# Attention scores of 64-feature heads: three half-height matmuls replaced by two full-height ones

## The chip, the cores and the metric

The kernel runs on one core of a Trainium2 chip. The metric is device time in microseconds (us) for one execution. The engines are named as in the profile: PE is TensorE (its weight loads are listed as PEld), DVE is VectorE, ACT is ScalarE, POOL is GpSimd, and SP is SyncE, whose queue issues the DMAs. All five run side by side, each works through its own instruction list strictly in the order written at build time, and semaphores make one wait for another.

## The reference, cut to what matters

Two blocks follow each other on 256 tokens of width 1024. The first block has two layers. Each layer projects the tokens (and 256 context tokens) with `w_in` and computes three kinds of attention, A, B and C. A has 32 features per head; B and C have 64, and they are what the change touches:

```
qb = axial_rope(rms_norm(qb.reshape(b, s, B_HEADS, HEAD_DIM), gqa_q_norm[l]), row, col)
kb = axial_rope(rms_norm(kb.reshape(b, s, B_KV_HEADS, HEAD_DIM), gqa_k_norm[l]), row, col)
yb = map_query_blocks(lambda q_blk: gqa_attend(q_blk, kb_all, vb_all), qb) * jax.nn.silu(gb)
qn = rms_norm(qn.reshape(b, s, C_HEADS, HEAD_DIM), nat_q_norm[l])
kn = rms_norm(kn.reshape(b, s, C_HEADS, HEAD_DIM), nat_k_norm[l])
yn = neighbourhood_attend(qn, kn, vn.reshape(b, s, C_HEADS, HEAD_DIM), kn_c, vn_c, nat_rpb[l], rows)
```

In layer 0 the context tokens attend too (to the context keys alone); in layer 1 they give only keys and values. B has six query heads on two key heads, C has six heads with a bias table `nat_rpb`. The second block (a gated MLP and a dilated attention) isn't touched.

## The kernel before

**Tiling.** Tokens come in four blocks of 128: blocks 0 and 1 are the tokens x, blocks 2 and 3 the context c. The columns of `w_in` are cut into seven slabs of 512 per layer: slabs 0 and 1 hold two A heads each, slabs 2 and 3 three B heads with their one key head, slabs 4 to 6 two C heads each. For each slab the code projects the blocks (`project`, which calls `mm3`) and then attends (`attend`), one block after the other. In layer 0 the loads and matmuls of `ada`, which make modulation vectors from `w_ada`, are spread between the slabs.

**Precision.** A 32-bit operand is held as a high part (rounded to the matmul's format) and a low part, the rest. A product takes three matmuls: high by high, low by high, high by low. `mm3` (L193 to L195) does so for the projections, at full height, that is with 128 rows of contraction. `scores` (L331) does so for one or two heads at a time, on the 64 rows where a head's features lie; two heads of a pair lie on rows 0 to 63 and 64 to 127 of the same tile.

**A projection's way to the scores.** `project` copies the matmul's result to `pj` (L472), makes the normalization factor on POOL (L202, L204), splits the values (`split_v`, L298 to L302), scales (L496), applies gains or the rotary tables (`times_tab`, L430 and L437, then L507), and has the result in `fin`. For B a POOL copy (L511) sets the key head a second time beside itself. Then two transposes (L517; three for a full B block) put features on rows, ACT casts the high parts out of PSUM (L522) and DVE subtracts to get the low parts (L523). A B slab's third query head has a tile of its own, `qx`, with one buffer, whose tag `aux` the C slabs' bias `rpb` shares.

**Softmax.** Two PSUM banks (`sc`) hold scores. DVE takes the maximum (L566; for C L560 and L561, which adds the bias), ACT exponentiates (L313) and rounds (L318), DVE makes the low part (L319), a DMA transposes the result (L321, tile `pt`), and PE multiplies with the values (L339 to L341).

**What sets the order.** In the first block a scheduler decides at build time in which order each engine gets its instructions; `urgent(40)` on `scores` raises their priority. The order is fixed when the kernel runs. Tiles with the same tag share their buffers, so a tile waits until the last use of the one whose buffer it takes.

**Tables.** The cosine and sine tables are loaded once, ahead of layer 0 (L673), and POOL multiplies them with the gains at the start of each layer (L705). `gates_of` loads the residual gate for a layer's output projection into a buffer of its own (`rowb`).

## Time and profile before

| | |
|---|---|
| time, median of 3 runs | 1182.47 us (1181.87 to 1186.19) |
| the profiled execution | 1193.97 us, of which 1192.3 us are its span |
| mean granted TensorE clock in it | 0.954 of full speed |
| PE busy | 1113.6 us (93%), 6600 matmuls |
| DVE, ACT, POOL busy | 837.6 us (70%), 610.5 us (51%), 465.8 us (39%) |
| the chain that ended last | 79% PE, 10% DMA, 5% DVE |
| score matmuls (L331) on that chain | 7% |

A busy time counts overlapping instructions of one engine once. A PE matmul's duration in the trace includes its latency, so how fast matmuls follow each other is read from their starts, not from their durations. The first block takes the span up to about 680 us; B and C slabs lie in about 178 to 400 us (layer 0) and 534 to 650 us (layer 1).

### The profile page before, as it was taken

How to read it: one execution, taken by the hardware profiler on the slowest of the kernel's cores; microseconds unless marked ns; L12 is line 12 of the kernel's file. 1: busy time of each engine (PE TensorE's matmuls, PEld its weight loads, DVE VectorE, ACT ScalarE, POOL GpSimd, SP SyncE). 2: the span in 40 equal slices, each digit the busy share in tenths (PEclk: the TensorE clock that was granted, in tenths of full speed). 3: DMA queues.
4: the chain of work that ended last, by engine and by line, in shares of the span. 5: the costliest groups of instructions: out<-in, count | busy, mean ns of one | idle time of the engine just before them, and what ended most of it. 6: DMA issues, size and time to landing. Idle time of an engine off the chain costs nothing.

```text
span 1192.3 us, 19339 instructions
## 1 busy us (share of the span) xinstructions
PE 1113.6 (93%) x6600; PEld 851.7 (71%) x6600; DVE 837.6 (70%) x1833; ACT 610.5 (51%) x1364; POOL 465.8 (39%) x698
## 2 busy tenths in 40 slices
PE   5988999898999989999997899999999999999996
PEld 1656657465676777777775688888778888888885
DVE  4467777775476677768876559765568888888783
ACT  2445564554364555566654354554446545555551
POOL 3476655341451039354361301000255555555520
PEclk9989989996999999789999899999989999999998
DMA  9355665878495535666766475555457666876652
GB/s 354 140 146 105 162 146 107 221 141 221 134 235 138 147 128 159 125 106 140 171 161 149 158 245 183 191 170 183 137 179 196 173 178 185 192 173 184 170 144 63
DMA packets 193971, 197.88 MB, mean 166 GB/s; under 512 B 150448, under 2 KB 154576, under 8 KB 193616
## 3 DMA queue, kind: packets, MB, share of 16 engines
q1 hardware_dynamic: 193872, 196.65, 62.0%
q8 instruction: 52, 0.85, 0.3%
q14 instruction: 47, 0.39, 0.1%
HBM read 158.84 MB, written 2.11 MB: 135 GB/s over the span
## 4 chain that ended last, share of the span: by engine, by line
PE 79%; DMA 10%; DVE 5%; issue 2%; ACT 2%; POOL 1%; SPq 0%; DVEq 0%; POOLq 0%; ACTq 0%
PE pj L193 17%; PE pj L194 17%; PE pj L195 16%; PE sc L331 7%; DMA pt<-pp 5%; PE ops L194 3%; PE ops L193 3%; PE ops L195 3%; PE po_bank L339 3%; DMA raw<-in_w_ada 2%; PE po_bank L341 2%; PE adaps L391 2%; DVE wlo L177 1%; PE po_bank L340 1%; PE tp L517 1%
## 5 line engine op out<-in xcount | busy, mean ns | idle before, releaser
L193 PE MATMUL pj<-whi,hxh 128*128 128x512 f32 (+1 forms) x800 | 317.3, 397 | 5.2 <-ACT hxh L271 4.3
L194 PE MATMUL pj<-whi,hxl 128*128 128x512 f32 (+1 forms) x800 | 309.6, 387 | 1.1 <-DVE hxl L255 0.7
L195 PE MATMUL pj<-wlo,hxh 128*128 128x512 f32 (+1 forms) x800 | 307.5, 384 | 0.0
L172 ACT CAST whi<-raw 128x1024 fp32r<-128x1024 f32 x224 | 235.0, 1052 | 139.8 <-DMA raw<-in_b_w_qk 32.5
L175 POOL TENSOR_TENSOR wlo<-raw,whi 128x512 fp32r<-128x512 f32 x130 | 181.6, 1418 | 149.6 <-ACT whi L172 146.5
L177 DVE TENSOR_TENSOR wlo<-raw,whi 128x1024 fp32r<-128x1024 f32 x159 | 202.2, 1275 | 53.5 <-ACT whi L172 52.1
L193 PEld LDWEIGHTS pj<-whi,hxh 128*128 128x128 f32 x800 | 154.3, 193 | 38.4 <-ACT hxh L271 5.0
L194 PEld LDWEIGHTS pj<-whi,hxl 128*128 128x128 f32 x800 | 154.3, 193 | 32.5 <-issue 2.6
L195 PEld LDWEIGHTS pj<-wlo,hxh 128*128 128x128 f32 x800 | 153.4, 192 | 30.3 <-issue 1.1
L313 ACT ACTIVATE pe<-sc,nm 128x512 f32<-128x512 f32 (+2 forms) x184 | 105.3, 576 | 106.9 <-DVE nm L566 51.9
L319 DVE SCALAR_TENSOR_TENSOR pp<-pe,pp 128x512 f16<-128x512 f32 (+3 forms) x152 | 114.8, 760 | 43.4 <-ACT pp L318 42.8
L331 PE MATMUL sc<-qk 64*128 64x256 f32 (+4 forms) x612 | 107.8, 355 | 4.6 <-ACT qk L522 1.9
L318 ACT ACTIVATE pp<-pe 128x512 f16<-128x512 f32 (+3 forms) x152 | 88.6, 590 | 43.2 <-DMA pt<-pp 42.4
L204 POOL TENSOR_TENSOR rs<-ms,mhalf 128x1 f32<-128x1 f32 (+3 forms) x98 | 92.4, 944 | 4.2
L331 PEld LDWEIGHTS sc<-qk 64*128 64x128 f32 (+1 forms) x612 | 64.3, 191 | 39.1 <-issue 13.9
L339 PEld LDWEIGHTS <-pt 128*128 128x128 f16 x544 | 54.0, 99 | 47.0 <-issue 23.2
L193 PE MATMUL pj<-whi,hch 128*128 128x512 f32 (+2 forms) x224 | 81.9, 367 | 0.5 <-ACT whi L172 0.5
L194 PE MATMUL pj<-whi,hcl 128*128 128x512 f32 (+2 forms) x224 | 81.6, 365 | 0.4 <-DVE hcl L255 0.4
L195 PE MATMUL pj<-wlo,hch 128*128 128x512 f32 (+2 forms) x224 | 80.2, 363 | 0.0
L339 PE MATMUL po_bank<-vt,pt 128*128 128x128 bf16 x400 | 67.5, 228 | 13.4 <-DMA pt<-pp 10.4
L341 PE MATMUL po_bank<-vt,pt 128*128 128x128 bf16 x400 | 66.9, 226 | 0.0
L566 DVE TENSOR_REDUCE nm<-sc 128x1 f32<-128x512 f32 (+1 forms) x96 | 54.1, 573 | 18.1 <-PE sc L331 17.6
(192 smaller groups left out, 1963.5 us busy)
## 6 DMA issues: line engine op xcount, KB each, us to landing
raw<-in_b_w_qk SPq DMA_DIRECT2D x64, 512.0 KB, 4.3
raw<-in_w_in SPq DMA_DIRECT2D x56, 512.0 KB, 4.6
raw<-in_w_ada SPq DMA_DIRECT2D x48, 512.0 KB, 4.9
raw<-in_a_w_in SPq DMA_DIRECT2D x48, 512.0 KB, 4.7
raw<-in_w_out SPq DMA_DIRECT2D x16, 512.0 KB, 4.4
raw<-in_a_w_out SPq DMA_DIRECT2D x16, 512.0 KB, 4.6
raw<-in_b_w_vz SPq DMA_DIRECT2D x16, 512.0 KB, 4.1
raw<-in_b_w_out SPq DMA_DIRECT2D x8, 512.0 KB, 3.9
```

The lines of the kernel that those rows point to most:

```text
L172: nc.scalar.copy(hi, raw)
L175: nc.gpsimd.tensor_tensor(lo[:, j], raw[:, j], hi[:, j].bitcast(F32), ALU.subtract)
L177: nc.vector.tensor_tensor(lo, raw, hi.bitcast(F32), ALU.subtract)
L193: nc.tensor.matmul(ps, h, whi[:, c0:c1], start=st, stop=False)
L194: nc.tensor.matmul(ps, l, whi[:, c0:c1], start=False, stop=False)
L195: nc.tensor.matmul(ps, h, wlo[:, c0:c1], start=False, stop=en)
L204: nc.gpsimd.tensor_tensor(rs[:, :n], ms[:, :n], mhalf[:, :n], ALU.pow)
L313: nc.scalar.activation(pe[:, c : c + w], ps, AF.Exp, bias=nm, scale=sign, accum_out=zz)
L319: nc.vector.scalar_tensor_tensor(pp[:, 1, :], pe, PSCALE, pp[:, 0, :], ALU.mult, ALU.subtract)
L331: nc.tensor.matmul(o, q[i == 2], k[i == 1], start=(i == 0), stop=(i == 2))
L339: nc.tensor.matmul(ps, pt[:, 0, i, :], v[:, 0:128], start=(i == 0), stop=False)
L341: nc.tensor.matmul(ps, pt[:, 1, i, :], v[:, 0:128], start=False, stop=(i == n - 1))
```

## The change

**Scores.** For B and C, `project` doubles each head's 64 features side by side before the transposes: ACT copies `fin` into the 512 columns of `pj`, each head twice (L531 of the new file). A transpose of 128 columns then gives one head on rows 0 to 63 and the same head on rows 64 to 127. There is one transpose per head (L533): four for a full block, one or two for a block that gives keys alone. ACT casts all of it out of PSUM (L534). For a key head DVE subtracts on all 128 rows (L535), so that the low part, tile `kl`, stands on both halves too. For a query head DVE subtracts on rows 64 to 127 alone (L538), so that the high part stands above the low part. `scores2` (L336 and L337) then multiplies this query tile by the keys' high parts and by their low parts, two matmuls of 128 rows, where there were three of 64. The fourth product, low by low, comes in with them. A keeps its form.

**Memory.** `qx` and the POOL copy L511 are gone; `kl` is new, with two buffers. To make room the rotary products work in place in `fin`, the cosine and sine tables are loaded in each layer into a shared `s512` buffer (L720), and the gate of `gates_of` shares the tag `aux` with the bias `rpb`.

In the built program the counts are: 216 score matmuls of 64 rows become 144 of 128 rows (of 512 columns 144 become 96, of 256 columns 72 become 48); 110 transposes become 164; ACT has 40 doubling copies more (30 of them 128x512), and 30 casts of 128x512 in place of ones of 128x256 and 128x128; DVE's subtractions there go from 68 to 86; POOL loses 16 copies; SP has four table loads in each layer in place of four in all.

```
-                qk = [wk.tile([P, 4, 2, P], F32R, tag="qk" + t, bufs=2, name="qk") for t in "hl"]
+                qk = wk.tile([P, 4, 4, P], F32R, tag="qk", bufs=2, name="qk")
                 qx = None
-                if kd == "B":
-                    qx2 = wk.tile([P, 2, 4, P], F32R, tag="aux", bufs=1, name="qx")
-                    qx = [qx2[:, i] for i in range(2)]
+                if kd == "A":
...
+                else:
+                    qx = wk.tile([P, 4, 1 if kd == "B" else 2, P], F32R, tag="kl", bufs=2, name="kl")
...
-                if kd == "B":
-                    nc.gpsimd.tensor_copy(fin[:, 256:320], fin[:, 192:256])
-                wins = (0, 192, 128) if kd == "B" else (0, 128)
...
+                nq = qw // 64
+                i0 = 0 if full else nq
+                two = pj.rearrange("p (h t d) -> p h t d", h=4, t=2)[:, i0:4]
+                heads = fin[:, 64 * i0 : 256].rearrange("p (h d) -> p h d", d=64)
+                nc.scalar.copy(two, heads.unsqueeze(2).to_broadcast([P, 4 - i0, 2, 64]))
+                for i in range(i0, 4):
+                    nc.tensor.transpose(tp[:, i, :], pj[:, i * P : (i + 1) * P], ident)
+                nc.scalar.copy(qk[:, blk, i0:4, :], tp[:, i0:4, :])
+                nc.vector.tensor_tensor(qx[:, blk], tp[:, nq:4, :], qk[:, blk, nq:4, :].bitcast(F32), ALU.subtract)
+                if full:
+                    ql = qk[64:128, blk, 0:nq, :]
+                    nc.vector.tensor_tensor(ql, tp[64:128, 0:nq, :], ql.bitcast(F32), ALU.subtract)
...
+    @urgent(40)
+    def scores2(o, q, kh, kl):
+
+        nc.tensor.matmul(o, q, kh, start=True, stop=False)
+        nc.tensor.matmul(o, q, kl, start=False, stop=True)
...
+                        if kd != "A":
+                            q = qk[:, blk, r0, :]
+                            scores2(
+                                sc_[:, :nk], q, qk[:, kb0:4, (192 if kd == "B" else 128) // 64 + vh, :], qx[:, kb0:4, vh, :]
+                            )
+                            continue
...
-                    scr.tile([P, D], F32, tag="rowb", bufs=1, name="gtb"), gd[l][i].rearrange("k p -> (k p)")
+                    wk.tile([P, D], F32, tag="aux", bufs=1, name="gtb"), gd[l][i].rearrange("k p -> (k p)")
...
-            for nm, w in (("cosA", 32), ("sinA", 32), ("cosB", 64), ("sinB", 64)):
-                t = tb_.tile([P, 2, w], F32, name=nm)
-                nc.sync.dma_start(t, a[nm])
-                consts[nm] = t
...
+                tabs, consts = {}, {}
+                cs4 = s512("cs").rearrange("p (t a d) -> p t a d", t=4, a=2)
+                for i, (nm, w) in enumerate((("cosA", 32), ("sinA", 32), ("cosB", 64), ("sinB", 64))):
+                    consts[nm] = cs4[:, i, :, :w]
+                    nc.sync.dma_start(consts[nm], a[nm])
```

**PE, layer 1, the heads of the second B slab's block 1.** Before, one of the pair's heads stands alone between projection matmuls (`pj<-`):

```order
L193 MATMUL pj<-whi,hxh 128x512
L194 MATMUL pj<-whi,hxl 128x512
L195 MATMUL pj<-wlo,hxh 128x512
L331 MATMUL sc<-qk 128x512 x3
L193 MATMUL pj<-whi,hxh 128x512
```

After, the pair's second head and the slab's third head at the same place:

```order
L336 MATMUL sc<-qk 128x512
L337 MATMUL sc<-kl,qk 128x512
L336 MATMUL sc<-qk 128x512
L337 MATMUL sc<-kl,qk 128x512
L193 MATMUL pj<-whi,hxh 128x512
```

Three matmuls a head have become two; they still stand between other work.

**ACT, layer 1, around the last C slab's projections** (`ev<-pj` is the copy out of the projection, `qk<-tp` the cast after the transposes, `pe` and `pp` the softmax). Before:

```order
L472 COPY ev<-pj 128x512
L477 ACTIVATE sq<-pj 128x256
L288 ACTIVATE hch<-yps 128x4x128
L318 ACTIVATE pp<-pe 128x512
L522 CAST qk<-tp 128x256
```

After, with the doubling copies (`ev<-fin`):

```order
L531 COPY ev<-fin 128x512
L313 ACTIVATE pe,z<-sc,nm 128x512 x2
L288 ACTIVATE hch<-yps 128x4x128
L318 ACTIVATE pp<-pe 128x512
L531 COPY ev<-fin 128x512
L318 ACTIVATE pp<-pe 128x512
L534 CAST qk<-tp 128x512 x2
```

A projection now passes ACT twice on its way to the scores, and softmax work stands between.

**POOL, start of layer 0** (`rs` is the normalization factor, `cosAt` to `sinBt` the tables times the gains). Before, from the table products on:

```order
L705 TENSOR_TENSOR cosBt<-cosB,gains 128x128 x2
L705 TENSOR_TENSOR sinBt<-sinB,gains 128x128 x2
L202 TENSOR_SCALAR ms<-ss 128x8
L204 TENSOR_TENSOR rs<-ms,mhalf 128x8
L300 TENSOR_TENSOR vr<-ev,vt 128x128
L491 TENSOR_TENSOR gate<-gate,gains 128x128
```

After:

```order
L300 TENSOR_TENSOR vr<-ev,vt 128x128
L725 TENSOR_TENSOR cosAt<-cs,gains 128x64 x2
L500 TENSOR_TENSOR gate<-gate,gains 128x128
L725 TENSOR_TENSOR sinAt<-cs,gains 128x64 x2
L725 TENSOR_TENSOR cosBt<-cs,gains 128x128 x2
L301 CAST vt<-vr 128x2x64
L725 TENSOR_TENSOR sinBt<-cs,gains 128x128 x2
L202 TENSOR_SCALAR ms<-ss 128x8
L500 TENSOR_TENSOR gate<-gate,gains 128x128
L302 TENSOR_TENSOR vt<-vr,vt 128x2x64
```

The eight table products have moved from ahead of the first projection's normalization to between the first and the second.

## Rows read from the trace of the kernel before

**Rows 1.** Windows: stretch, length, busy PE, PEld, DVE, ACT, POOL, clock, DMA share, GB/s.

```profile
178.00:400.00 222.00, 205.39 (x1266) 146.04 (x1265) 146.94 (x394) 110.47 (x283) 78.97 (x129) 0.93 0.70 168
534.00:650.00 116.00, 110.69 (x779) 84.75 (x778) 91.58 (x242) 68.76 (x167) 46.12 (x88) 0.99 0.69 160
```

**Rows 2.** PE's waits, 100 to 660 us: us in total, times, longest us.

```profile
PE po_bank L339 <- DMA pt<-pp: 10.4, 11, 2.3
PE adaps L391 <- DMA raw<-in_w_ada: 8.5, 7, 2.0
...
PE tp L517 <- DVE qk L523: 2.2, 1, 2.2
...
PE sc L331 <- ACT qk L522: 1.4, 2, 1.2
```

**Rows 3.** PE in order of time, one head between projection matmuls: start us, us.

```profile
574.20 0.40 PE L195 MATMUL pj<-wlo,hxh 128*128 128x512 f32 x1
574.52 0.96 PE L331 MATMUL sc<-qk 64*128 64x512 f32 x3
575.41 0.50 PE L193 MATMUL pj<-whi,hxh 128*128 128x512 f32 x1
575.75 0.39 PE L194 MATMUL pj<-whi,hxl 128*128 128x512 f32 x1
```

**Rows 4.** The same view, a pair issued together.

```profile
553.75 0.49 PE L331 MATMUL sc<-qk 64*128 64x512 f32 x1
553.76 0.49 PE L331 MATMUL sc<-qk,qx 64*128 64x512 f32 x1
...
554.65 0.50 PE L193 MATMUL pj<-whi,hxh 128*128 128x512 f32 x1
```

**Rows 5.** The same view, two heads one behind the other.

```profile
251.25 0.96 PE L331 MATMUL sc<-qk,qx 64*128 64x512 f32 x3
252.05 0.85 PE L331 MATMUL sc<-qk 64*128 64x512 f32 x3
```

**Rows 6.** The same view, a context head of 256 columns.

```profile
233.72 0.62 PE L331 MATMUL sc<-qk,qx 64*128 64x256 f32 x3 [0.23 <-ACT pe L313]
234.26 0.50 PE L195 MATMUL pj<-wlo,hch 128*128 128x512 f32 x1
```

**Rows 7.** The same view, four transposes between projection matmuls.

```profile
52.98 0.39 PE L195 MATMUL pj<-wlo,hch 128*128 128x512 f32 x1
53.21 0.60 PE L244 MATMUL hps<-ident,xh 128*128 128x128 f32 x4
53.56 0.48 PE L193 MATMUL pj<-whi,hch 128*128 128x512 f32 x1
53.88 0.39 PE L194 MATMUL pj<-whi,hcl 128*128 128x512 f32 x1
```

**Rows 8.** Groups by shape, ACT and DVE: count, busy us, mean ns.

```profile
L522 ACT CAST qk<-tp 128x256 fp32r<-128x256 f32 x42 | 15.5, 371 | 19.6 <-PE tp L517 19.4
L254 ACT CAST hch<-hf 128x512 fp32r<-128x512 f32 x8 | 4.9, 618 | 2.3 <-DVE hf L250 2.3
L523 DVE TENSOR_TENSOR qk<-tp,qk 128x256 fp32r<-128x256 f32 x42 | 17.4, 415 | 3.0 <-ACT qk L522 2.9
```

**Rows 9.** POOL in order of time, start of layer 0.

```profile
43.10 0.60 POOL L705 TENSOR_TENSOR cosAt<-cosA,gains 128x64 f32<-128x64 f32 x2
...
45.23 1.05 POOL L705 TENSOR_TENSOR sinBt<-sinB,gains 128x128 f32<-128x128 f32 x2
54.82 0.20 POOL L202 TENSOR_SCALAR ms<-ss 128x8 f32<-128x8 f32 x1 [8.55 <-DVE ss L479]
```

**Rows 10.** DVE in order of time, end of layer 1.

```profile
644.63 0.49 DVE L561 CUSTOM_DVE_ANT_0 sc<-sc,rpb,m 128x256 f32<-128x256 f32 x1
...
651.18 1.30 DVE L642 TENSOR_TENSOR ops<-ops,gtb 128x512 f32<-128x512 f32 x2 [1.65 <-PE ops L195]
```

**Rows 11.** DMA issues: KB each, median us to landing.

```profile
gtb<-gd SPq DMA_DIRECT2D x3, 512.0 KB, 5.4
```

More of the change, by code (lines that the diff above doesn't have):

```diff
@@ L291, in y_to_act, with split_v @@
         )
-    def split_v(dst, src, wk, eng=nc.vector):
+    def split_v(dst, src, wk, eng=nc.vector, vrw=256):
         w = src.shape[-1]
@@ L442, in slab_state @@
                 vw = 64 if kd == "B" else 128
-                qk = [wk.tile([P, 4, 2, P], F32R, tag="qk" + t, bufs=2, name="qk") for t in "hl"]
+                qk = wk.tile([P, 4, 4, P], F32R, tag="qk", bufs=2, name="qk")
                 qx = None
-                if kd == "B":
-                    qx2 = wk.tile([P, 2, 4, P], F32R, tag="aux", bufs=1, name="qx")
-                    qx = [qx2[:, i] for i in range(2)]
+                if kd == "A":
+                    qk = qk.rearrange("p b h q -> p (b h q)").rearrange("p (i b a q) -> p i b a q", i=2, b=4, a=2)
+                    qk = [qk[:, i] for i in range(2)]
+                else:
+                    qx = wk.tile([P, 4, 1 if kd == "B" else 2, P], F32R, tag="kl", bufs=2, name="kl")
                 vt = wk.tile([P, 4, vw // 64, 3, 64], BF16, tag="vt", bufs=2, name="vt")
@@ L492, in project @@
                     gates[blk] = gt_
-                split_v(vt[:, blk : blk + 1], pj[:, 256:cg], wk, nc.gpsimd)
+                split_v(vt[:, blk : blk + 1], pj[:, 256:cg], wk, nc.gpsimd, P)
                 qn = pj
@@ L496, in project @@
                 nc.vector.tensor_tensor(qv, qv, rs.unsqueeze(2).to_broadcast([P, ng, d]), ALU.mult)
-                fin = wk.tile([P, 320], F32, tag="fin", bufs=2, name="fin")
+                fin = wk.tile([P, 256], F32, tag="fin", bufs=2, name="fin")
                 if strm == "x" and kd != "C":
-                    t1 = wk.tile([P, 256], F32, tag="t1", bufs=1, name="t1")
                     t2 = wk.tile([P, 256], F32, tag="t2", bufs=1, name="t2")
-                    times_tab(nc.vector, kd, t1, qn, tabs["cos", kd][:, tb])
+                    times_tab(nc.vector, kd, fin, qn, tabs["cos", kd][:, tb])
                     times_tab(nc.gpsimd, kd, t2, qn, tabs["sin", kd][:, tb])
@@ L506, in project @@
                     for i in range(2):
-                        nc.vector.tensor_tensor(hv(fin, i), hv(t1, i), hv(t2, 1 - i), ALU.add)
+                        nc.vector.tensor_tensor(hv(fin, i), hv(fin, i), hv(t2, 1 - i), ALU.add)
                 else:
                     times_tab(nc.vector, kd, fin, qn, gtab[kd], full)
-                if kd == "B":
-                    nc.gpsimd.tensor_copy(fin[:, 256:320], fin[:, 192:256])
-                wins = (0, 192, 128) if kd == "B" else (0, 128)
@@ L513, in project @@
                 tp = bank("tr", "tp", (P, 4, P))
-                b0 = 0 if full else 1
-                for i, c in enumerate(wins):
-                    if i == 1 or full:
-                        nc.tensor.transpose(tp[:, i, :], fin[:, c : c + P], ident)
-                parts = [(tp[:, b0:2, :], [t[:, blk, b0:2, :] for t in qk])]
-                if kd == "B" and full:
-                    parts.append((tp[:, 2, :], [t[:, blk, :] for t in qx]))
-                for src, (hi, lo) in parts:
-                    nc.scalar.copy(hi, src)
-                    nc.vector.tensor_tensor(lo, src, hi.bitcast(F32), ALU.subtract)
+                if kd == "A":
+                    b0 = 0 if full else 1
+                    for i in range(b0, 2):
+                        nc.tensor.transpose(tp[:, i, :], fin[:, i * P : (i + 1) * P], ident)
+                    hi, lo = (t[:, blk, b0:2, :] for t in qk)
+                    nc.scalar.copy(hi, tp[:, b0:2, :])
+                    nc.vector.tensor_tensor(lo, tp[:, b0:2, :], hi.bitcast(F32), ALU.subtract)
+                    return
@@ L536, in attend @@
                 elif kd == "B":
-                    prs = [[(0, qk, 0), (64, qk, 0)], [(0, qx, 0)]]
+                    prs = [[(0, None, 0), (1, None, 0)], [(2, None, 0)]]
                 else:
-                    prs = [[(0, qk, 0), (64, qk, 1)]]
+                    prs = [[(0, None, 0), (1, None, 1)]]
                 for ip, pr in enumerate(prs):
@@ L547, in attend @@
                             sc_[:, :nk],
-                            [t[r, blk, 0, :] if qt is qk else t[r, blk, :] for t in qt],
+                            [t[r, blk, 0, :] for t in qk],
                             [t[r, kb0:4, 1, :] for t in qk],
                         ))
-                        scs.append(sc_)
                     scores(us)
```

5 lines of the change are left out of this document (2 added, 3 removed).

## The prediction

> **What bounds the kernel now.** I read the windows first: in the two stretches where B and C slabs lie, PE is busy 205.4 of 222 us and 110.7 of 116 us, DVE 66% and 79%, ACT 50% and 59% [rows 1]. So PE sets the pace there, and what ends its idle time comes second: 10.4 us for the transposed probabilities, 8.5 us for `w_ada` loads, and little for the projections' way to the scores, 2.2 us for DVE's subtraction and 1.4 us for ACT's cast, out of 560 us [rows 2]. Hence PE's own time is to be counted, and a busy time doesn't do for that, because durations include latency. I went to PE's order of time and took starts. Projection matmuls of 512 columns follow each other in 0.23 us (52.98 to 53.21) [rows 7]. A head's three score matmuls take far more than 3 x 0.23: from the projection matmul before them to the second one behind them 574.20 to 575.75, 1.55 us, of which two projection matmuls account for 0.46. The head costs 1.09 us, 0.40 more than its columns [rows 3]. A pair issued together costs no more: its two first matmuls start 0.01 us apart, and 0.90 us later the next work starts (553.75 to 554.65) against 0.89 alone [rows 4, 3]. And where two heads follow each other, in another bank and with other weights, the second begins 0.80 us after the first, not 0.89 [rows 5]. So the extra time isn't paid at a new head; it sits where 64-row and 128-row work meet, about 0.1 us at each of four starts (the start of the group, its second matmul, the first projection matmul behind it and the second): 0.32, 0.34 in place of 0.23 [rows 3].
>
> **PE, what goes.** There are 72 heads of B and C: 48 with 512 columns (144 matmuls by three) and 24 with 256. In the trace's order I counted how they stand. Of the 48, 32 run alone, as in [rows 3], and 16 as 8 pairs, as in [rows 4]; of the 24, 12 alone, as in [rows 6], and 12 as 6 pairs. Since only two `sc` banks exist and they come free one after the other, most pairs aren't issued as pairs. After the change a head costs two full-height matmuls, and if 128 rows follow 128 rows without a gap, as in projections, that is 0.46 us (0.23 for 256 columns).
> - 512 columns alone: 1.09 - 0.46 = 0.63. About a third of these heads stand right behind value matmuls, where not all of the gap shows, so I take 0.55: 32 x 0.55 = 17.6.
> - 512 columns, pair: 0.90 and the same 0.2 of gaps at its ends, less 4 x 0.23: 0.18, taken as 0.13: 8 x 0.13 = 1.0.
> - 256 columns alone: 0.54 (233.72 to 234.26) [rows 6] and 0.2, less 0.23: 0.51, taken as 0.45: 12 x 0.45 = 5.4. A pair: 0.74 - 0.46 = 0.28, taken as 0.25: 6 x 0.25 = 1.5.
>
> Together 25.5 us.
>
> **PE, what comes.** 54 transposes more. Four between projection matmuls take 53.21 to 53.88, less one matmul, 0.44, so 0.11 each [rows 7]: 5.9 us. PE's net is 25.5 - 5.9 = 19.6 us, 12.7 in layer 0 (16 heads and 4 pairs of 512, all of 256, 32 transposes) and 6.9 in layer 1 (16 heads, 4 pairs, 22 transposes).
>
> **How much of it the end sees.** Layer 0: PE is busy for 0.93 of the stretch, and a shorter PE meets the same transposed probabilities and `w_ada` loads [rows 1, 2], so I take 0.7: 8.9 us. Layer 1: DVE is at 79% there and gets more work; I take half, 3.5 us. Together 12.4.
>
> **ACT and DVE.** Per full block the doubling copy is 0.62 us (a 128x512 cast from SBUF), the wider cast 0.62 in place of 0.37, the extra subtraction about 0.42 [rows 8]; with two more transposes (0.22) the way from `fin` to the scores grows by 0.62 + 0.25 + 0.42 + 0.22 = 1.5 us. In sum about 26 us on ACT and 10 us on DVE over 340 us, where ACT has 159 us idle [rows 1]. What hides it is the projection matmuls that PE has queued: now only 2.2 and 1.4 us of waits show at this place [rows 2]. So I cost it at nothing beyond the shares above. If that cover is gone, it is the slower rival. The POOL copy that goes saves B some latency, also hidden.
>
> **Tables.** At the start of layer 0 the eight table products run from 43.10 to 46.28 and POOL then idles 8.55 us for the first normalization [rows 9]. Now their loads stand behind `lamv` on SP and the products between the first and the second normalization: 3.2 us (45.23 + 1.05 - 43.10) that POOL doesn't have to spare, before the second context block and both x blocks can go on. Cost 0 to 4 us, taken 2.5, since PE has some projections left. In layer 1 the same on a PE with more matmuls queued: 0 to 4, taken 1.5. The loads queue ahead of `w_in` loads, which is in the 4.
>
> **Bias and gate in one buffer.** The last gate load of layer 1 now waits for the last use of the bias, 644.63 to 645.12, and lands 5.4 us later at 650.5 [rows 10, 11]; its first use is at 651.18 [rows 10]. Hidden by 0.7 us; its 512 KB run beside the last probabilities: 0 to 3, taken 0.5. In layer 0 the gate is first used behind a whole output projection's matmuls. The B slabs no longer share a buffer with the bias: 0 to 2 us gained, taken 0.
>
> **Sum.** 12.4 - 2.5 - 1.5 - 0.5 = 7.9. The profiled execution took 1193.97 us (1192.3 of span), 11.5 above the median of the three runs; the terms are far from the ends of the span and hold for either, so I take them off the median: 1182.47 - 7.9 = **1174.5 us**.
>
> **The rivals.**
> - **The gaps stay** (the change doesn't do what it says). If they belong to score matmuls and not to height, only the count is left: 0.23 x 32 + 0.115 x 12 less, 0.23 x 8 + 0.115 x 6 more for the pairs that ran side by side: 6.2 us, against 5.9 for transposes. With the 4.5 of tables and gate: 1182.5 + 4.2 = 1187. [rows 5] speaks against it. The Trainium skill, TensorEngine Tiling (Array Packing), Overview, gives up to twofold speed for a contraction of 64 rows or fewer and so speaks for pairs and against the change. By that rule alone this rival's 1187 would come out. The trace agrees for a pair that is issued together [rows 4], not for the heads that run alone.
> - **Eaten by the next bound.** DVE in layer 1 and the probabilities' DMAs in layer 0 leave 0.4 of 19.6: 7.8 - 4.5 = 3.3, 1179. For it: DVE at 79% [rows 1]. Against: PE's small waits [rows 2].
> - **The longer way shows** (slower). The place is ACT's list: a doubling copy that waits for DVE holds back the exponentials behind it, so `sc` banks come free late and PE starves. 30 full blocks x 1.5 = 45 us if all shows. With half of it: 1174.5 + 22.5 = 1197. It turns the result to slower by over 0.5% once 0.31 of it shows (13.9 of 45). For it: ACT's list now mixes both, and the order was rearranged throughout the first block. Against: 3.6 us of waits in 560 us at this place now [rows 2].
>
> **How the numbers follow.** Forecast 0.58, gaps stay 0.07, eaten 0.21, longer way 0.14. A measurement of this kernel tells about 0.5% (5.9 us) from no change: below 1176.6 is faster, above 1188.4 slower. The forecast lies close to the first bound, so I count 0.02 of it as no change; rivals one and two are no change, the third is slower. Hence faster 0.56, same 0.30, slower 0.14. The range: at the low end all of PE's 19.6 us and 2 from the freed buffer with no cost, 1161, rounded down to 1160; at the high end it takes in the first two rivals and the first part of the third: 1190.
>
> **What would show it right or wrong.** In the trace after: two score matmuls of 128 rows with 0.46 us between the work around them, no 0.32 and 0.34 starts beside them, and four transposes in 0.44; PE's sum of these 19 to 20 us less. The windows of layer 0's B and C slabs should shorten by some 9 us, those of layer 1 by 3 to 4, the first 180 us lengthen by 2 to 3. The table products should show on POOL between two normalizations. It is wrong if score groups keep their gaps, if PE's waits for DVE's subtraction or ACT's cast grow from 3.6 us to over 10, or if the first 180 us alone lose as much as the slabs win.

## The result and the profile after

The change made the kernel slower by 0.6%: the median of 20 runs is 1190.11 us against 1184.53 us of 20 runs of before beside them, ratio 1.0057 with a 95% interval of 1.0032 to 1.0083. The prediction was 1174.5, 8 us under the median it started from.

The profiled execution of after took 1193.46 us (span 1191.7), 3 us over its median. That of before in [rows 1 to 11] took 1193.97, 9 us over its own. So I compare after with a second profile of before too (b_same below, 1177.19 us), which lies 7 us under that median, and rest nothing on a span alone.

Windows of after, which answer to [rows 1] (stretch, length, busy PE, PEld, DVE, ACT, POOL, clock, DMA share, GB/s):

```profile
178.00:400.00 222.00, 192.13 (x1209) 144.84 (x1208) 150.57 (x395) 119.31 (x285) 74.81 (x112) 0.94 0.68 166
534.00:650.00 116.00, 103.50 (x757) 84.37 (x756) 94.02 (x245) 73.02 (x173) 45.88 (x84) 0.96 0.66 157
```

The same windows in the second profile of before:

```profile
178.00:400.00 222.00, 206.94 (x1309) 149.43 (x1309) 148.54 (x399) 112.08 (x286) 77.24 (x126) 0.96 0.70 172
534.00:650.00 116.00, 106.23 (x716) 80.94 (x715) 87.47 (x215) 63.65 (x143) 43.84 (x74) 0.97 0.66 154
```

PE is busy 14.8 us less in the first stretch. Part of that is work that has gone, but PE also starts 100 matmuls fewer there, where the change takes away only 16 in all of layer 0 (48 score matmuls less, 32 transposes more): it is behind. Who ends its waits is in PE's waits, 100 to 660 us, of after (us in total, times, longest us), which answer to [rows 2]:

```profile
PE po_bank L345 <- DMA pt<-pp: 17.2, 13, 4.9
PE adaps L396 <- DMA raw<-in_w_ada: 13.1, 8, 2.7
PE tp L533 <- ACT ev L531: 4.5, 4, 2.0
PE sc L336 <- ACT whi L172: 3.4, 1, 3.4
...
PE sc L336 <- ACT qk L534: 1.6, 1, 1.6
```

and of the second profile of before:

```profile
PE adaps L391 <- DMA raw<-in_w_ada: 9.1, 7, 2.1
PE po_bank L339 <- DMA pt<-pp: 8.1, 11, 2.1
PE po_bank L339 <- DVE ov L572: 2.5, 2, 1.3
PE sc L331 <- ACT qk L522: 2.3, 2, 2.1
```

The waits for probabilities are twice those of the second profile (10.4 us in the first [rows 2]), and ACT ends waits that were not there: for the doubling copy (L531) and for a weight cast (L172). PE's own work did shrink in the way predicted. PE in order of time, one head between projection matmuls (start us, us), for [rows 3]: 0.46 us from 541.98 to 542.44, no gap beside it.

```profile
541.75 0.39 PE L195 MATMUL pj<-wlo,hxh 128*128 128x512 f32 x1
541.98 0.39 PE L336 MATMUL sc<-qk 128*128 128x512 f32 x1
542.21 0.39 PE L337 MATMUL sc<-kl,qk 128*128 128x512 f32 x1
542.44 0.39 PE L193 MATMUL pj<-whi,hxh 128*128 128x512 f32 x1
...
596.27 0.40 PE L336 MATMUL sc<-qk 128*128 128x512 f32 x1
596.50 0.40 PE L337 MATMUL sc<-kl,qk 128*128 128x512 f32 x1
596.74 0.40 PE L336 MATMUL sc<-qk 128*128 128x512 f32 x1
596.97 0.40 PE L337 MATMUL sc<-kl,qk 128*128 128x512 f32 x1
597.21 0.60 PE L533 MATMUL tp<-ident,ev 128*128 128x128 f32 x4
```

Two heads, one behind the other, take 0.94 us (596.27 to 597.21). The same view, four transposes, and two heads behind value matmuls:

```profile
553.88 0.61 PE L533 MATMUL tp<-ident,ev 128*128 128x128 f32 x4
554.25 0.48 PE L194 MATMUL pj<-whi,hxl 128*128 128x512 f32 x1
...
573.35 0.48 PE L336 MATMUL sc<-qk 128*128 128x512 f32 x1
573.67 0.40 PE L337 MATMUL sc<-kl,qk 128*128 128x512 f32 x1
574.52 0.50 PE L336 MATMUL sc<-qk 128*128 128x512 f32 x1 [0.46 <-ACT pe L313]
574.86 0.40 PE L337 MATMUL sc<-kl,qk 128*128 128x512 f32 x1
```

The transposes take 0.37 us to the next start, before 0.35 [rows 7]. In the last rows the two heads are split: the second waits 0.46 us, since ACT has not yet read out its bank. Such waits are not new (3.2 us in after, in five places; 1.5 us in the second profile of before, in four).

What stands on the way, groups by shape (count, busy us, mean ns), for [rows 8]:

```profile
L531 ACT COPY ev<-fin 128x512 f32<-128x512 f32 x30 | 18.7, 622 | 11.4 <-DVE fin L435 5.6 <-POOL vr L300 2.7 <-DVE gate L496 1.8
L534 ACT CAST qk<-tp 128x512 fp32r<-128x512 f32 x30 | 17.8, 595 | 7.9 <-PE tp L533 7.8
L538 DVE TENSOR_TENSOR qk<-tp,qk 64x256 fp32r<-64x256 f32 x18 | 7.7, 428 | 0.4
```

When the first and the last scores of each layer start, in us, from PE's order of time, and the rows of PE's waits from 60 to 655 us added up by what ended them:

| profile | layer 0 | layer 1 | between | probabilities | raw loads | ACT | DVE | sum |
|---|---|---|---|---|---|---|---|---|
| before | 67.0 to 385.3 | 466.1 to 643.7 | 80.8 | 10.4 | 10.4 | 5.9 | 13.3 | 40.0 |
| before, second | 64.9 to 375.7 | 456.0 to 627.4 | 80.3 | 8.1 | 11.0 | 6.0 | 15.2 | 40.3 |
| after | 64.5 to 378.7 | 466.3 to 640.2 | 87.6 | 17.2 | 14.9 | 18.9 | 5.7 | 56.7 |
| b_house | 65.7 to 373.1 | 461.7 to 627.8 | 88.6 | 17.0 | 11.9 | 9.2 | 9.3 | 47.4 |
| b_two | 66.8 to 377.7 | 458.4 to 622.8 | 80.7 | 12.0 | 12.2 | 8.2 | 21.1 | 53.5 |
| b_two_tr | 66.2 to 375.0 | 454.3 to 620.2 | 79.3 | 8.5 | 11.3 | 7.9 | 20.0 | 47.7 |
| a_copyf | 63.2 to 373.9 | 461.1 to 636.9 | 87.2 | 14.7 | 13.6 | 14.4 | 13.6 | 56.3 |
| a_dbl | 66.0 to 386.9 | 477.3 to 653.8 | 90.4 | 20.0 | 11.1 | 13.6 | 21.5 | 67.7 |
| a_rows | 63.8 to 388.2 | 477.9 to 660.9 | 89.7 | 10.1 | 13.0 | 11.3 | 10.6 | 45.0 |

(The sum of a_dbl holds 1.5 us for POOL besides.) PE's time came down by some 12 us (below) and its waits went up by 16.

The granted clock differs between these executions, and a length takes it in. So here are three stretches with it: layer 0 from its first to its last scores; from there to the last matmul of layer 0's output projection (`ops`), with the same matmuls in every kernel; and from there to the last scores of layer 1. Each cell gives the length in us, the mean granted clock, and their product in whole us. The product is an estimate of the length at full clock; it takes PE as busy wherever the clock is low.

| profile | layer 0 | to the last `ops` | to layer 1's last scores |
|---|---|---|---|
| before | 318.2 x 0.914: 291 | 38.9 x 1.000: 39 | 219.6 x 0.938: 206 |
| before, second | 310.8 x 0.934: 290 | 38.7 x 1.000: 39 | 213.0 x 0.968: 206 |
| after | 314.2 x 0.940: 295 | 45.5 x 0.925: 42 | 216.0 x 0.929: 201 |
| b_house | 307.4 x 0.961: 295 | 45.2 x 0.962: 43 | 209.6 x 0.967: 203 |
| b_two | 310.9 x 0.934: 290 | 39.1 x 1.000: 39 | 206.1 x 0.967: 199 |
| b_two_tr | 308.9 x 0.945: 292 | 39.5 x 0.957: 38 | 205.7 x 0.959: 197 |

The lengths of the two profiles of before add up to 577 and 563 us, their products agree within 1 us. After loses 4 to 5 us in layer 0 and 3 behind it, and wins 5 in layer 1. From the last scores to the end it takes 551.5 us, before 548.5 and 548.1. The experiments ask why.

### The profile page after: what moved, and what is told of

Same layout as the page of the kernel before. It is cut to its first block, busy times and chain, and to the rows that moved or that the text cites. A ratio compares the mean times of both kernels' runs of the same rounds, so it can differ in the third digit from the quotient of the medians.

```text
span 1191.7 us, 19318 instructions
## 1 busy us (share of the span) xinstructions
PE 1095.4 (92%) x6582; PEld 854.3 (72%) x6582; DVE 848.6 (71%) x1851; ACT 630.9 (53%) x1392; POOL 465.7 (39%) x682
## 5 line engine op out<-in xcount | busy, mean ns | idle before, releaser
L172 ACT CAST whi<-raw 128x1024 fp32r<-128x1024 f32 x224 | 234.7, 1052 | 137.6 <-DMA raw<-in_b_w_qk 31.3
L195 PE MATMUL pj<-wlo,hxh 128*128 128x512 f32 (+1 forms) x800 | 307.4, 384 | 0.0
L319 DVE SCALAR_TENSOR_TENSOR pp<-pe,pp 128x512 f16<-128x512 f32 (+3 forms) x152 | 118.9, 787 | 42.1 <-ACT pp L318 41.6
L318 ACT ACTIVATE pp<-pe 128x512 f16<-128x512 f32 (+3 forms) x152 | 88.4, 590 | 39.8 <-DMA pt<-pp 39.1
L345 PE MATMUL po_bank<-vt,pt 128*128 128x128 bf16 x400 | 66.3, 225 | 18.9 <-DMA pt<-pp 17.2
L194 PE MATMUL pj<-whi,hcl 128*128 128x512 f32 (+2 forms) x224 | 80.3, 358 | 0.3 <-DVE hcl L255 0.3
L347 PE MATMUL po_bank<-vt,pt 128*128 128x128 bf16 x400 | 65.4, 223 | 0.0
L331 PE MATMUL sc<-qk 64*128 64x128 f32 (+3 forms) x432 | 60.7, 330 | 3.7 <-ACT pe L313 2.1
L346 PE MATMUL po_bank<-vt,pt 128*128 128x64 bf16 x400 | 62.9, 196 | 0.0
L587 DVE TENSOR_REDUCE nm<-sc 128x1 f32<-128x512 f32 (+1 forms) x96 | 53.5, 572 | 11.2 <-PE sc L331 6.4
```

The source lines that it names most:

```text
L172: nc.scalar.copy(hi, raw)
L194: nc.tensor.matmul(ps, l, whi[:, c0:c1], start=False, stop=False)
L195: nc.tensor.matmul(ps, h, wlo[:, c0:c1], start=False, stop=en)
L318: nc.scalar.mul(pp[:, 0, :], pe, PSCALE)
L319: nc.vector.scalar_tensor_tensor(pp[:, 1, :], pe, PSCALE, pp[:, 0, :], ALU.mult, ALU.subtract)
L331: nc.tensor.matmul(o, q[i == 2], k[i == 1], start=(i == 0), stop=(i == 2))
```

## The experiments

"Order held" means: the program is built as it stands, and behind the scheduler single instructions are edited, while every engine keeps its order and its waits. "Own order" means that the scheduler saw the edit and ordered anew. All ratios are to the kernel before in runs on the same chip, with 95% intervals. Edits are cut to what matters, and some lines are condensed.

### Before again, and the housekeeping alone

> The kernel before, unchanged, to have a second profile of it and the size of what repeats. Its first profiled execution (1193.97 us) lay 9.4 us over the median of its 20 runs (1184.53). Every theory expects a ratio of 1.000 within 0.3%. If the granted clock explains the spread between executions, runs of one kernel should line up: about 0.7 us shorter for each 0.001 of mean clock, as the 20 runs of the changed kernel do (0.952 with 1197.7 us, 0.974 with 1179.9 us).

0.9996 (0.9965 to 1.0027). Its profile is the second one of before.

b_house, own order, the kernel before with:

```
-            consts = {}                       (loads ahead of the layers)
+                cs4 = s512("cs").rearrange("p (t a d) -> p t a d", t=4, a=2)
-                    scr.tile([P, D], F32, tag="rowb", bufs=1, name="gtb")
+                    wk.tile([P, D], F32, tag="aux", bufs=1, name="gtb")
-                    times_tab(nc.vector, kd, t1, qn, ...)
+                    times_tab(nc.vector, kd, fin, qn, ...)
```

> The kernel before with the change's housekeeping alone: tables loaded per layer into the shared s512 buffer, the gate in the buffer of the bias, rotary products in place, a narrower buffer in the values' split. Scores and transposes stay as before. Housekeeping theory (the terms of 2.5, 1.5 and 0.5 us in the prediction, or more): slower than before by 4 us or more, 1188 to 1192. Theory of the longer way, and theory of the order and the clock: within 3 us of before, 1182 to 1188.

1.0006 (0.9976 to 1.0036): as a whole the housekeeping alone costs nothing that can be told. But its trace shows a cost where I had put none. The gate `gtb` now has to wait for the last use of the bias in layer 0 too. In the second profile of before its load was issued long before (SP's queue):

```profile
291.86 0.33 SPq L276 DMA_DIRECT2D gtb<-gd  x1
386.73 0.33 SPq L276 DMA_DIRECT2D gtb<-gd  x1
```

and DVE's first product with it ran at 374.98. In after, SP:

```profile
380.39 0.33 SPq L276 DMA_DIRECT2D gtb<-gd  x1
384.06 3.72 SPq L321 DMA_TRANSPOSE pt<-pp  x2
397.71 0.33 SPq L276 DMA_DIRECT2D gtb<-gd  x1
```

DVE (in order of time) in after:

```profile
383.32 0.68 DVE L319 SCALAR_TENSOR_TENSOR pp<-pe,pp 128x512 f16<-128x512 f32 x1
384.01 1.90 DVE L663 TENSOR_TENSOR ops<-ops,gtb 128x512 f32<-128x512 f32 x3
385.81 0.68 DVE L319 SCALAR_TENSOR_TENSOR pp<-pe,pp 128x512 f16<-128x512 f32 x1
...
386.88 1.87 DVE L664 TENSOR_TENSOR yc<-res,ops 128x512 f32<-128x512 f32 x3
```

The products (L663) start when the gate has landed (383.99), and the sums behind them (L664) free the three banks that projections write, each of which holds a result by then. Until then PE has no `ops` matmul that can start: the next one comes at 388.15, when the second sum ends. In the second profile of before fifteen of them, from 379.15 on, cover the waiting for probabilities at this place. In after the values of the last pair's first head stand next in PE's list, and the wait for their probabilities lies open. The products don't lengthen this wait: the first head's low part (383.32) stands ahead of them, and its transpose, issued at 384.06, lands at 387.10. PE in after:

```profile
387.15 0.29 PE L345 MATMUL po_bank<-vt,pt 128*128 128x128 bf16 x1 [4.86 <-DMA pt<-pp]
...
388.15 0.78 PE L193 MATMUL ops<-whi,hch 128*128 128x512 f32 x1
```

in the second profile of before:

```profile
378.32 0.23 PE L339 MATMUL po_bank<-vt,pt 128*128 128x128 bf16 x1 [0.86 <-DMA pt<-pp]
...
379.15 0.48 PE L193 MATMUL ops<-whi,hch 128*128 128x512 f32 x1
```

and at the same place in b_house:

```profile
382.30 0.29 PE L339 MATMUL po_bank<-vt,pt 128*128 128x128 bf16 x1 [4.40 <-DMA pt<-pp]
```

In the windows of after around it the granted clock falls to 0.50 (the 1.2 GHz level) behind a stretch in which PE was busy 2.65 of 6.80 us; in both profiles of before it stays at 1.00 up to the last `ops`:

```profile
372.50:379.50 7.00, 7.00 (x37) 5.68 (x35) 3.98 (x14) 3.37 (x8) 0.00 (x0) 1.00 0.33 46
379.50:386.30 6.80, 2.65 (x34) 2.07 (x32) 5.92 (x18) 3.84 (x9) 0.00 (x0) 0.99 0.58 141
386.30:393.00 6.70, 5.85 (x24) 4.79 (x25) 3.10 (x7) 2.17 (x6) 0.75 (x2) 0.50 0.63 165
```

So from layer 0's last scores to its last `ops` matmul it takes 45.5 us in after and 45.2 in b_house, in place of 38.9 and 38.7: 6 to 7 us more. All twelve profiles with the housekeeping have 44.4 to 47.8 us there and 7.0 to 9.1 us of PE's waits, the eight without it 38.7 to 39.9 and 2.3 to 3.5. The column "between" of the first table is no measure of this: in both kernels it holds 23 projection matmuls of layer 1 more ahead of the first scores, which is work moved and not added.

b_house's time doesn't show the cost, and the clock is part of the reason. Its 12 runs have a mean granted clock of 0.967, the 29 of before beside them 0.960, and among before's runs on one chip 0.001 more clock goes with 0.5 to 0.7 us less time. As an estimate from these numbers, 3 to 5 us are hidden so; the products in the second table add up to 541 us for b_house and 535 to 536 for before. Why its clock is higher isn't shown. The changed kernel's loss isn't a lower clock: its 20 runs have 0.961, those of before 0.956 to 0.960 on the five chips of the experiments.

### The longer way

a_nocopy (own order) leaves the doubling copy out; a_copyf (order held) lets it write 64 columns, so that the copies on ACT take 9.8 us in place of 22.3. The edit of a_nocopy:

```
-                nc.scalar.copy(two, heads.unsqueeze(2).to_broadcast([P, 4 - i0, 2, 64]))
-                    nc.tensor.transpose(tp[:, i, :], pj[:, i * P : (i + 1) * P], ident)
+                    nc.tensor.transpose(tp[:, i, :], fin[:, min(64 * i, P) : min(64 * i, P) + P], ident)
```

> The changed kernel without the doubling copy on ACT: each transpose takes a 128-column window of the rotated heads that begins at its head (the last one begins one head earlier), so the lower 64 rows hold a neighbour's features and not the head's own. All else, the number of transposes, casts, subtractions and matmuls, stays. Theory of the longer way: 0.6 us less on the way of each of 30 full blocks and some 20 us less on ACT, so at least a third of 18 us comes back: 1184 or less. Housekeeping theory and theory of the order and the clock: within 3 us of the changed kernel, 1187 to 1193.

1.0007 (0.9978 to 1.0035), 6 us under the changed kernel by the ratios.

> The changed kernel with every engine's order held: the doubling copies on ACT write 64 columns instead of 512, 256 or 128; the transposes then take what stood in pj, not the heads. ACT loses some 0.45 us in each of 30 full blocks, 15 us in sum, and the way to the scores gets that much shorter. Theory of the longer way as a cost of its own: 4 us or more under the changed kernel, at or below 1.002 of before. Theory of the order: the instructions' order is what costs, not the copy's length: within 2 us of the changed kernel, 1.004 to 1.007 of before.

1.0049 (1.0012 to 1.0085), 1 us under it. The same copy, taken out ahead of the scheduler, seems to give 6 us, and made short behind it, 1 us (the intervals overlap a little). In the table's row PE's waits for ACT fall by 4.5 us and those for DVE rise by 7.9.

b_way (order held) puts work of that size into the kernel before, two more casts from `tp` into a spare tile ahead of L522:

> The kernel before with every engine's order held, and the way to the scores made longer: ahead of each 128x256 cast out of PSUM in the B and C blocks (30 of them) ACT runs two more casts of 128x140 into a spare tile, 0.25 us each: 0.5 us per block, 15 us of ACT in sum, about the doubling copy. Theory of the longer way as a cost of its own: 4 us or more over before (1.003 or more). Theory of the order, and my prediction, which put this at nothing: within 2 us of before.

1.0020 (0.9980 to 1.0060): 2 us, within -2 to 7.

a_dbl (own order) takes the copy's place with a broadcast in DVE's last step:

```
-                        nc.vector.tensor_tensor(hv(fin, i), hv(fin, i), hv(t2, 1 - i), ALU.add)
+                            nc.vector.tensor_tensor(two[:, :, :, i * (d // 2) : (i + 1) * (d // 2)],
+                                tw(hv(fin, i)), tw(hv(t2, 1 - i)), ALU.add)
```

> The changed kernel with the doubling done by DVE's last step instead of an ACT copy: the rotary sum (or the product with the gains) is written twice side by side into pj with a broadcast input. One instruction less on the way, 40 ACT copies less (some 20 us of ACT), DVE's writes are 512 columns instead of 256 (some 0.27 us per block more, 10 us of DVE). Theory of the longer way (the copy): as without the copy, where the median was 1182.8: 1181 to 1186. If it is the DVE that now sets the pace: 1190 or more. Theory of the late tables: 1188 to 1191, since those stay.

1.0172 (1.0132 to 1.0212), 14 us worse than the changed kernel, though ACT is busy 17 us less (613.4 in place of 630.9). PE's waits, 100 to 660 us:

```profile
PE po_bank L345 <- DMA pt<-pp: 20.4, 20, 3.0
...
PE tp L548 <- DVE ev L533: 7.2, 4, 3.5
PE yps L285 <- DVE qk L553: 5.6, 1, 5.6
```

DVE is busy 14 us more (863.0 in place of 848.6), and PE now waits for it; the order is another one too, and the run doesn't part the two.

### PE's side of the change

a_three (own order) issues the second score matmul twice:

```
+        nc.tensor.matmul(o, q, kl, start=False, stop=False)
         nc.tensor.matmul(o, q, kl, start=False, stop=True)
```

> The changed kernel with its second score matmul (by the keys' low parts) issued twice, so three full-height matmuls for a head: 48 of 512 columns and 24 of 256 more, 48 x 0.23 + 24 x 0.12 = 14 us of PE's own time. It doubles the low part in the scores. If PE's time sets the end of the B and C slabs, as the prediction took it for 0.5 to 0.7 of them: 7 to 10 us over the changed kernel, 1197 to 1200. If something else ends the waits there (probabilities, loads): under 4 us, 1190 to 1194.

1.0133 (1.0089 to 1.0177): 9 of 14 us show, within 3 to 15 by the intervals.

b_less and a_less (order held) take a score matmul away, b_less from each of the 72 heads, a_less from the 50 whose two stand next to each other; its waits go to the neighbour in the same bank. In short:

```
 for i in b.instructions:
+    if score(i) and not i.start_tensor_calc and not i.stop_tensor_calc:
+        held[bank(i)] = waits(i); continue
```

> The kernel before with every engine's order held: behind the scheduler, the middle one of the three score matmuls of each B and C head (high by low) is taken out. It leaves that product out of the scores. PE's own time falls by about 13 us (40 x 0.25 for 32 single heads and 8 pairs of 512 columns, 3 for those of 256), two thirds of what the change gives, and nothing else changes. Theory that PE sets the pace (the prediction's 0.5 to 0.7): 7 to 9 us faster than before, 1172 to 1175. Theory of the next bound (what PE saves turns into waits for the probabilities): at most 3 us, 1178 to 1182.

0.9959 (0.9928 to 0.9989): 4.8 of about 13 us, within 1 to 9.

> The changed kernel with every engine's order held: where a head's two score matmuls stand next to each other (50 heads, 33 of them of 512 columns), the second (by the keys' low parts) is taken out, so the scores lack it. PE's own time falls by 33 x 0.23 + 17 x 0.12 = 9.6 us. Theory that PE sets the pace: 5 to 7 us under the changed kernel (1.0057 of before), so 0.0 to 0.1% from before, 1183 to 1185. Theory of the next bound: under 2 us from the changed kernel, 1188 to 1190.

1.0034 (1.0001 to 1.0066): 2.7 of 9.6 us, though the intervals exclude neither nothing nor the double. Both lean to the next bound, and neither excludes the prediction's shares. So the full change of PE's work, order held, came next: b_two gives the two remaining matmuls all 128 rows, b_two_tr adds 54 transposes, and a_rows does the reverse in the changed kernel.

```
+    i = again(i, ins=tuple(tall(p) for p in i.ins), tile_size=(128, 128), tile_position=(0, 0))
```

> The kernel before with every engine's order held, and the change's matmuls alone: of the three score matmuls of a B or C head the second goes, and the two others take all 128 rows (the other 64 rows hold another head's features, so the scores are not the reference's). No copy, no transposes more, no tables moved. By the prediction's prices PE loses 25.5 us. Theory that PE sets the pace, with the prediction's shares (0.7 in layer 0, 0.5 in layer 1): 15 to 17 us faster than before, ratio 0.986. Theory of the next bound (a third, as the middle matmul alone gave 4.8 of 13 us): 8 to 9 us faster, ratio 0.993.

0.9966 (0.9940 to 0.9991): 4 us (the medians, 1174.34 and 1182.15, are 8 apart). PE's waits rise from 40.3 to 53.5 us, in before's own order.

> The kernel before with every engine's order held, two full-height score matmuls for a head as in b_two (the scores are not the reference's), and 54 transposes issued twice, as many as the change adds (both of a C block, one of a full B block): PE's side of the change in full, and nothing else of it. By the prediction's prices PE gets 5.9 us over b_two, net 19.6 us under before. Prediction's shares: 12.4 us faster than before, ratio 0.990. Theory of the next bound (what is taken away comes back by a fifth to a third, what is added costs four fifths, as a_rows showed): 3 to 5 us over b_two, ratio 0.999 to 1.001. If it stays at b_two (0.9966), the transposes cost nothing and the rest of the change, 0.9%, is order and tables.

0.9892 (0.9853 to 0.9931) on 6 runs: 12.8 us faster, the number of the prediction's shares and not that of the next bound. More work on PE than in b_two, and a shorter time: the waits are 47.7 in place of 53.5, which covers the transposes, but not the 8 us beyond. The two ran on different chips, each beside its own runs of before. The mean granted clock doesn't part them (0.964 and 0.965), and their profiled executions lie only 1.7 us apart, so the traces don't settle it: the difference stays open. Both say that PE's side alone makes the kernel faster.

> The changed kernel with every engine's order held, and its matmuls undone alone: three matmuls of 64 rows for a head in place of two of 128, all on rows 0 to 63 (the one for the queries' low parts takes their high parts again, so the scores are not the reference's). PE gets some 30 us more (26 single heads of 512 columns x 0.63, 10 pairs x 0.87, 12 single heads of 256 x 0.5, 6 pairs x 0.64, less what stands behind value matmuls). Theory that PE sets the pace: 17 to 20 us over the changed kernel, ratio 1.020 to 1.023. Theory of the next bound: about 10 us over it, ratio 1.013 to 1.015. If it is under 3 us, the matmuls bring nothing in this order.

1.0260 (1.0216 to 1.0304): 24 us over the changed kernel. PE's starts add up to 24 us more in its trace. So in the changed order, too, the two full-height matmuls are worth what they save. And everything else about the changed program costs 2.6% against before, of which some 14 us are PE's by its starts (transposes, and pairs that don't run side by side here).

### The order

The same instructions as before, other priorities of the score matmuls (own order):

```
-    @urgent(40)
+    @urgent(100)      (b_u100;  b_s120: 120)
     def scores(units):
```

> The kernel before with the same instructions in another order: the priority of the score matmuls is 100 instead of 40, which moves rows on every engine from the first slab on. No cost of the change is in it. Theory of the order and the clock: an order as such is worth 0.5% either way, so it differs from before by over 4 us. Theories of named costs: within 3 us of before, 1179 to 1185.

1.0033 (1.0005 to 1.0061): another order alone, 4 us.

> The kernel before, every instruction the same, with priority 120 instead of 40 for the score matmuls: another order and nothing else (priority 100 gave 1.0033). Theory of the order: an order by itself is worth some 0.3% in either direction, so 0.996 to 1.000 or 1.003 and more is possible, and with 0.997 or less it beats both kernels. Theory that the order matters only together with the change's costs: within 0.15% of before.

1.0008 (0.9979 to 1.0037). And the changed kernel's instructions in other orders: a_early writes layer 1's preparation ahead of layer 0's output projection, a_prio changes priorities, a_klprio does so too and loads the tables into a buffer of `kl`.

```
                 if l == 0:
+                    nxt = setup(1)            (a_early: gains, lambda, tables)
                     for blk in (2, 3):
```
```
-    @urgent(40)     def scores2               +    @urgent(100)   (a_klprio: 200)
-    @urgent(80)     def pv                    +    @urgent(40)
+                with tc.high_priority(150):   (copy, transposes, cast, subtractions)
-                cs4 = s512("cs").rearrange(...)
+                cs4 = wk.tile([P, 4, 2, P], F32R, tag="kl", bufs=2, name="cs")...    (a_klprio)
```

> The changed kernel with layer 1's preparation (gains, lambda, the table loads into s512 and the table products) written ahead of layer 0's output projection, so that its s512 buffers come up before those of the normalized rows of layer 1. In the changed kernel the table products of layer 1 ran at 442.8 to 449.1 us, behind the second normalization of an x block, and the first scores of layer 1 came 87.6 us after the last ones of layer 0, in the kernel before 80.3 to 80.8. Theory of the late tables: that stretch falls back to 80 to 82 us, and the time by 4 to 8 us, to 1182 to 1186. Theory of the longer way alone: the stretch shortens, but the probabilities and ACT eat it, 1188 to 1191. Theory of the order and the clock: anything within 6 us of 1190, with no tie to that stretch.

1.0137 (1.0083 to 1.0191). The theory of late tables fell: the stretch between the layers was 84.8 us, 2.8 less, and the kernel 9 us slower than the changed one.

> The changed kernel with the same instructions in another order, by priorities alone: 100 instead of 40 for the score matmuls, 40 instead of 80 for the value matmuls, 150 for the doubling copy, the transposes, the cast and the subtractions. Theory of the order (the changed program's order is a poor one, by no named cost): away from the changed kernel by over 3 us, downward if the way to the scores stands too late in it, 1182 to 1187. Theory that named costs make up the loss, whatever the order: within 3 us of the changed kernel, ratio 1.004 to 1.008.

1.0053 (1.0026 to 1.0080): no change by the ratio.

> The changed kernel with the tables of each layer loaded into a free buffer of the keys' low parts (tag kl) instead of an s512 buffer, so that layer 1's products don't queue behind the buffers of its normalized rows, and with priorities of the same kind (200 for scores, 40 for value matmuls, 150 for the way to the scores). Theory of late tables plus order: layer 1's first scores come 80 to 83 us after layer 0's last ones (87.6 in the changed kernel), and the time falls to or under that of before, 1173 to 1181. If only the stretch shortens and the time stays over 1185, the late tables were not part of the loss.

1.0022 (0.9992 to 1.0051), level with before. But the stretch between the layers is 87.1 us, though layer 1's table products now run from 360.5 us on (442.7 in after; 362.5 in a_early): it isn't the tables that fill it.

a_dbl with a_early's edit came out at 1.0154 (1.0111 to 1.0196):

> Both: layer 1's preparation early, and the doubling by DVE's last step. If the late tables and the copy are two separate costs, their gains add: 1174 to 1180, faster than the kernel before (1181 to 1184). If they cover one another: the better of the two, 1182 to 1185.

Neither expectation held: the two gains didn't add, and there was no gain in either edit.

So the same work takes from 1.0022 to 1.0137 of before in four orders of the changed program, and from 1.0000 to 1.0033 in three orders of before. No kernel that forms all products of the scores beats before.

## Why the prediction was wrong, point by point

- **What bounds the kernel.** "PE sets the pace" was true for work added (a_rows 24 of 24 us, a_three 9 of 14). For work taken away the runs disagree: 4.8 of 13 (b_less), 2.7 of 9.6 (a_less) and 4 of about 18 us (b_two) came back, but all of 11.5 in b_two_tr. PE at 93% with small waits says that others are just behind, not how far.
- **PE, what goes: the mechanism right, 25.5 us too much.** By starts in the traces, at full clock and with waits taken out, B and C's score matmuls went from 47.4 to 32.9 us, and the long starts of projection matmuls beside scores from 7.4 to 3.7 (nearly all that is left stands beside A's heads): 18.2 us. I had given each of 44 lone heads gaps on both sides; in before only 18 projection matmuls ahead of B and C's heads and 18 behind them hold the next start off.
- **The rival "the gaps stay" fell.** Beside full-height heads 4 of 55 projection matmuls hold the next start off to over 0.28 us at full clock, in before 36 of 47 beside half-height ones. The Trainium skill, TensorEngine Tiling (Array Packing), Overview, gives up to twofold speed where a dimension is 64 or less, and so speaks for pairs on 64 rows. The trace agrees that these gained least, 0.94 us now against 0.90 and 0.2 of gaps [rows 4].
- **What comes.** 54 transposes: 6.7 us (51.7 to 58.4 for all transposes) against 5.9. Net 11.5, not 19.6.
- **How much the end sees.** 12.4 was forecast. b_two_tr measured 12.8 (8 to 17) for PE's side in before's order, b_two 4 (1 to 7). If b_two_tr is right, the number came out because two misses cancelled: the net was 11.5 and not 19.6, and all of it showed and not 0.63; that is luck. By the second table, one profile each, the two shares were the wrong way round. Layer 0, where 8.9 us were to go, takes 290 and 292 us with PE's side alone and 295 as changed, against 290 to 291; layer 1, where 3.5 were to go, is 7 to 9 us shorter with PE's side alone and 5 as changed.
- **ACT and DVE at nothing.** With the order held the copy's length is worth little (1 us in a_copyf, 2 in b_way). But I asked only if PE would wait for cast and subtraction. The waits for the copy and the cast are 6.1 us (L531 and L534), under the 10 that I had set; the probabilities (4.9 us of them in the gate's stretch) and ACT's weight casts (L172) grew too. ACT's list holding back others is the third rival's mechanism, and it had the sign right. Its price isn't borne out: two runs moved a part of the way by itself, and the time moved by 1 and 2 us. No run isolates the rest.
- **Tables.** Layer 0: the products came between two normalizations on POOL, as forecast, and cost nothing visible in place of 2.5 us; the first scores start at 64.5 (67.0 and 64.9 before). For the 1.5 us of layer 1 no run shows a cost either: a_early and a_klprio moved its products 80 us ahead, and the stretch kept 84.8 and 87.1 us.

```profile
51.94 0.20 POOL L202 TENSOR_SCALAR ms<-ss 128x8 f32<-128x8 f32 x1 [9.87 <-DVE ss L488]
54.23 1.30 POOL L725 TENSOR_TENSOR cosAt<-cs,gains 128x64 f32<-128x64 f32 x2
...
58.81 0.20 POOL L202 TENSOR_SCALAR ms<-ss 128x8 f32<-128x8 f32 x1
```

- **Bias and gate in one buffer: wrong place.** I costed the end of layer 1 (0.5 us) and waved layer 0 through, as the gate's first use stands "behind a whole output projection's matmuls". But that projection is spread among the last slab's heads: in before the first product with the gate ran at 374.98, ahead of the last scores. The late load leaves PE 4.9 us without cover there, and 6.7 us at half clock follow (in before 3.4 us at half clock stand later, ahead of layer 1's scores): 6 to 7 us up to the last `ops`. At the end of layer 1 nothing shows: its last scores lie 26.3 us ahead of the last `ops` in after as in both profiles of before. How much of the 6 to 7 us reaches the end isn't settled, since b_house has it too, at a higher clock.
- **The step that failed** is the sum's cost side: 4.5 us for tables and gate, and nothing for ACT, DVE and the gate in layer 0. Between b_two_tr, which has PE's side alone, and the changed kernel lie 1.6% (20 us, 14 to 25); from b_two 0.9% (11 us). Shown of it: the 6 to 7 us behind layer 0's last scores, by a term that I had put at nothing, and waits that move from releaser to releaser when one is shortened. The rest is argued and not shown: it goes with the longer way and with the order that the scheduler gives the changed program, for which my prediction had no term. Four orders of the changed program differ by up to 1.1%. How the rest divides between the two stays open: a way that the scheduler sees can't be taken out without the order changing.
- **Range and chances.** The median lies 0.1 us over the range's upper end. Slower had 0.14, all of it for one mechanism; that the gain could come out and the costs be several times too small had none.

## What to carry to other kernels

Before a buffer is shared, look up in the order of the trace (not in the code) when the moved load was issued and when its first use ran: a scheduler pulls uses far ahead. Where the engine that paces has others just behind it, count what it loses at a fifth to the full (here 4 of 18 to 12.8 of 11.5 us), and what the edit adds elsewhere at the full. Read lengths beside the granted clock: two profiles of one kernel differed by 14 us in the same stretches, and by 1 with the clock taken in. And where a scheduler orders the program, an edit's price has a part that no row of before shows; here it was of the size of the gain.

## What the runs showed of the hardware

- The first full-height score matmul behind value matmuls holds the next one off by 0.32 us (573.35 to 573.67), behind projection matmuls by 0.23.
- One program, twelve times on one chip (b_same), goes from 1171.8 to 1185.4 us, with mean granted clocks of 0.966 and 0.957.
- Work that is taken out of a full list of PE turns into waits in part: in b_two PE's waits rose by 13 us where some 18 went, in b_two_tr by 7.
